# Attention outputs with values as weights, two heads side by side

## The chip, the cores and the metric

The kernel runs on one core of one Trainium2 chip. A core has TensorE (matrix products, PE in the rows), VectorE (DVE), ScalarE (ACT), GpSimd (POOL) and SyncE (SP), which starts most transfers. Each engine works through its own queue in order and waits on semaphores for the others. The metric is the device time of one execution in microseconds; lower is better.

## The reference

A trunk of two layers over 256 latent and 256 context tokens of width 1024. Each layer mixes the tokens in three groups of heads (a state space layer, latent attention, an mLSTM), projects them together (w_out), and then runs 64 experts. The attention group, cut to its core:

```python
def _attend(q_nope, q_rope, k_nope, k_rope, v):
    s = (jnp.einsum('bqhd,bkhd->bhqk', q_nope, k_nope)
         + jnp.einsum('bqhr,bkr->bhqk', q_rope, k_rope))
    p = jax.nn.softmax(s.astype(jnp.float32) * MLA_SCALE, axis=-1).astype(v.dtype)
    return jnp.einsum('bhqk,bkhd->bqhd', p, v)
...
    out_lat = ...          # 256 latent queries over 512 keys (context and latent)
    out_ctx = ...          # 256 context queries over 256 keys, layer 0 only
```

There are 8 heads; a head has 64 + 32 columns of query and key and 64 of value. All is float32.

## The kernel before, in words

A layer is a row of stages. The mixer first projects all inputs; then three generators run woven into each other: `a` is attention (`mla`, L859), `m` the mLSTM (`mlstm`), and `e` the products of a later modulation (`ada_pair`), which stream 1 MB weight tiles from memory. In one round of `weave` (L1379) `a` and `m` take two steps and `e` one; a step is what lies between two `yield`s. The compiler's scheduler then orders the instructions on each engine, and that order is fixed when the program runs. When all three are through, `post` multiplies by w_out (L1429) and the experts follow.

Attention works on items: one head and one segment of 256 queries. A segment has two tiles of 128 queries; the latent one (seg 1) has four tiles of 128 keys, the context one (seg 0) two. In layer 0 there are 16 items, in layer 1 eight (latent only). An item goes through three steps, spread over three turns of the loop at L953:

- `scores` (L906): two products of queries by keys into PSUM, VectorE's maximum along each row (L919), ScalarE's exponential with its row sum (L920), VectorE's reciprocal of the two sums (L921).
- `turn` (L923): TensorE turns each 128 x 128 block of the probabilities (tile `pr` into `pt`), VectorE copies the first query tile out of PSUM and ScalarE the second (L930).
- `outs` (L932): for each key tile and query tile a product with the turned probabilities as weights (128 columns) and the head's 64 value columns moving (L937). The result has queries along the partitions, so the reciprocal sum is one number in each partition: VectorE scales one tile (L944), ScalarE the other (L942), into `on`.

At the end (L970 to L974) the 16 blocks of `on` (8 in layer 1) are turned and copied into `cat`, which w_out reads with features along the partitions.

Names in the rows beside these: `ada` is `e`'s product, four column tiles of the array side by side, each with 32 columns of weights; `st`, `sT`, `mb`, `num`, `int`, `E`, `nd` and `ek` are the mLSTM's (`E` its decay tile of 128 x 512, made from `mb`); `gu` and `dn` are an expert's products; `hT` and `kkT` are other transposes. Transposes stand under L313, the helper `tpose`.

Of the kernel before, what the change touches and what calls it, by code (L numbers as in the profile page):

```python
# [10 lines left out]
F32 = mybir.dt.float32  # L11
BF16 = mybir.dt.bfloat16
I32 = mybir.dt.int32
AF = mybir.ActivationFunctionType
OP = mybir.AluOpType
# [256 lines left out]
class Trunk:  # L272
# [586 lines left out]
    def mla(self, l, qn, kn, kr, mp, cat, last):  # L859
        nc, d, v = self.nc, self.d, self.nc.vector  # L860
# [3 lines left out]
        for j in range(4):  # L864
            (v.tensor_copy if j % 2 else nc.scalar.copy)(kh[j][64:96], kr[64:96])
        V = mp.tile([128, 4, 512], F32, name="V")
        on = mp.tile([128, 4, 512], F32, name="on")
        qh = {}

        def values(i):  # L870
# [28 lines left out]
        def keys(hp):  # L899
            ps = self.bank("kh")  # L900
            nc.tensor.matmul(ps, wkv[:, hp * 128:hp * 128 + 128], kn, start=True, stop=True)
            k2 = kh[2 * (hp % 2):2 * (hp % 2) + 2]
            nc.scalar.copy(k2[0][0:64], ps[0:64])
            v.tensor_copy(k2[1][0:64], ps[64:128])

        def scores(it):  # L906
            h, seg = it["h"], it["seg"]
            nk = it["nk"]
            n = nk * 128
            it["pr"] = pr = mp.tile([128, 2, NT], F32, name="pr", bufs=2)  # L910
            it["sm"] = sm = mp.tile([128, 2, 4], F32, name="sm", bufs=4)
            both = self.bank("s") if nk == 2 else None
            for t in range(2):
                qt = seg * 2 + t
                ps = both[:, t * n:(t + 1) * n] if both is not None else self.bank("s")
                nc.tensor.matmul(ps, qh[h][:, qt * 128:(qt + 1) * 128], kh[h % 4][:, :n], start=True, stop=True)
                it[t] = ps
            for t in range(2):
                v.tensor_reduce(out=sm[:, t, 0:1], in_=it[t], axis=AX.X, op=OP.max, negate=True)  # L919
                nc.scalar.activation(pr[:, t, :n], it[t], AF.Exp, bias=sm[:, t, 0:1], accum_out=sm[:, t, 1:2])  # L920
            v.reciprocal(sm[:, :, 2:3], sm[:, :, 1:2])  # L921

        def turn(it):  # L923
            nk = it["nk"]
            it["pt"] = pt = mp.tile([128, 4, 2, 128], F32, name="pt", bufs=2)
            for t in range(2):
                pp = self.bank("pt")
                for kt in range(nk):
                    self.tpose(pp[:, kt * 128:(kt + 1) * 128], it["pr"][:, t, kt * 128:(kt + 1) * 128])
                (nc.scalar.copy if t else v.tensor_copy)(pt[:, 0:nk, t], pp[:, :nk * 128].rearrange("p (k q) -> p k q", k=nk))  # L930

        def outs(it):  # L932
            h, seg, nk = it["h"], it["seg"], it["nk"]
            po = self.bank("o")
            for kt in range(nk):
                for t in range(2):
                    nc.tensor.matmul(po[:, t * 64:(t + 1) * 64], it["pt"][:, kt, t], V[:, kt, h * 64:(h + 1) * 64],  # L937
                                     start=kt == 0 and t == 0, stop=kt == nk - 1 and t == 1)
            for t in range(2):
                o, a, sc = on[:, seg * 2 + t, h * 64:(h + 1) * 64], po[:, t * 64:(t + 1) * 64], it["sm"][:, t, 2:3]  # L940
                if t:
                    nc.scalar.activation(o, a, AF.Identity, scale=sc)  # L942
                else:
                    v.tensor_scalar(out=o, in0=a, scalar1=sc, scalar2=None, op0=OP.mult)  # L944

        queries(0)
        yield
# [1 line left out]
        for i in range(4):  # L949
            values(i)  # L950
        yield
        items = [dict(h=h, seg=seg, nk=4 if seg else 2) for h in range(8) for seg in ((1,) if last else (1, 0))]
        for n in range(len(items) + 2):  # L953
            if n < len(items):
                h = items[n]["h"]
                if h != items[n - 1]["h"] or n == 0:
                    if h == 4:
                        queries(1)
                        yield
                    if h % 2 == 0 and h < 6:  # L960
                        keys(h // 2 + 1)
                scores(items[n])
                yield
            if 1 <= n <= len(items):
                turn(items[n - 1])
                yield
            if n >= 2:
                outs(items[n - 2])
                yield
        for qt in range(2 if last else 0, 4):  # L970
            ps = self.bank("oT")
            for b in range(4):
                self.tpose(ps[:, b * 128:(b + 1) * 128], on[:, qt, b * 128:(b + 1) * 128])
            (nc.scalar.copy if qt % 2 else v.tensor_copy)(cat[:, 0:4, qt * 128:(qt + 1) * 128], ps.rearrange("p (b n) -> p b n", b=4))  # L974
            yield


# [266 lines left out]
    def mixer(self, l):  # L1244
# [131 lines left out]
        extra = late(extra, pace("late", l, 0))  # L1376
        ml = late(ml, pace("latem", l, 0))
        st = {"m": (ml, x), "a": (mla, y), "e": (extra, z)}
        weave(*(st[k] for k in pace("Do", l, "mae")))  # L1379
        self.dbg(f"cat5{l}", cat5)  # L1380
# [701 lines left out]
```

## Time and profile before

| | us |
|---|---|
| median of three runs | 1956.65 (1954.27 to 1961.2) |
| the profiled execution | 1952.31 |
| its span, first to last instruction | 1950.3 |
| mean granted clock of TensorE | 0.962 |
| TensorE busy | 1792.0 (92%) |
| VectorE busy | 775.7 (40%) |
| ScalarE busy | 394.1 (20%) |

The rows come from the profiled execution. A float32 matmul stands in them as two passes, each with its own weight load (PEld), so the trace counts 320 where the program has 160; a transpose stands as one. Busy time of TensorE holds the time in which a result is still on its way through the array, so the start of the next matmul tells more than the end of this one. The attention stretch of layer 0 ends at 304.2 us, where w_out begins, that of layer 1 at 1337.6.

### The profile page before, as it was taken

The page shows a single profiled execution, that of the slowest core. Times are in us where ns is not written, and L with a number is a line of the kernel's source. Part 1 is how long each engine was busy: PE and PEld are TensorE (multiplying, and loading weights), DVE is VectorE, ACT ScalarE, POOL GpSimd, SP SyncE. Part 2 cuts the span into 40 slices and gives each one's busy share as a digit, 9 for nine tenths or more (in the row PEclk, how much of TensorE's full clock was granted, in tenths as well). Part 3 has the DMA queues.
Part 4 walks back from the last instruction along what each step waited for, and adds up shares of the span by engine and source line. Part 5 has one row for each costly group of instructions (what it writes and reads, how often), then busy time and mean ns, then how long its engine had stood idle before and what let it go on. Part 6 is the DMA issues. An engine that isn't in the chain of part 4 may idle for free. (4 is left out here: it accounts for less than half of the span.)

```text
span 1950.3 us, 29070 instructions
## 1 busy us (share of the span) xinstructions
PE 1792.0 (92%) x10161; PEld 843.7 (43%) x10161; DVE 775.7 (40%) x2252; ACT 394.1 (20%) x756; POOL 453.5 (23%) x453
## 2 busy tenths in 40 slices
PE   6999999979999999999998089899899999999993
PEld 2654665533443433334332056665544444444330
DVE  5656664852422332222221386564722222322113
ACT  2345332301111111111111143531311111011000
POOL 3120211232232232223221570002011111112223
PEclk8999999989999999999999589899899999999997
DMA  8442568299999899999997425258599999996882
GB/s 327 143 98 102 180 242 304 81 337 348 342 335 336 323 304 350 371 352 350 341 365 269 130 74 107 97 217 307 189 417 366 350 345 332 340 370 200 320 296 88
DMA packets 158305, 523.98 MB, mean 269 GB/s; under 512 B 28862, under 2 KB 42110, under 8 KB 149452
## 3 DMA queue, kind: packets, MB, share of 16 engines
q1 hardware_dynamic: 139612, 480.36, 66.6%
q0 software_dynamic: 18544, 41.73, 9.7%
q8 instruction: 82, 1.34, 0.3%
q14 instruction: 67, 0.55, 0.1%
HBM read 531.12 MB, written 47.51 MB: 297 GB/s over the span
## 5 line engine op out<-in xcount | busy, mean ns | idle before, releaser
L1822 PE MATMUL gu<-ring,xT 128*32 128x512 f32 (+3 forms) x2896 | 653.4, 599 | 8.7 <-DMA ring<-in_exp_w 8.6
L1822 PEld LDWEIGHTS gu<-ring,xT 128*32 128x32 f32 (+3 forms) x2896 | 194.2, 128 | 372.0 <-issue 313.0
L1835 PE MATMUL dn<-ring,hT 128*32 128x512 f32 (+3 forms) x1448 | 319.2, 598 | 1.3 <-DVE hT L1726 1.0
L1845 POOL DMA_INDIRECT Y<-xo,gi x79 | 119.9, 1518 | 557.9 <-DMA Y<-xo,gi 129.0
L1718 DVE TENSOR_TENSOR hh<-gu,sg 128x256 f32<-128x256 f32 (+3 forms) x86 | 36.4, 425 | 496.5 <-ACT sg L1717 496.4
L1835 PEld LDWEIGHTS dn<-ring,hT 128*32 128x32 f32 (+3 forms) x1448 | 98.7, 128 | 178.3 <-issue 159.7
L1845 POOL DMA_INDIRECT Y<-xo,si x66 | 90.1, 1365 | 318.0 <-DMA Y<-xo,gi 216.5
L1840 DVE TENSOR_SCALAR xo<-dn,gc 128x512 f32<-128x512 f32 (+3 forms) x80 | 60.1, 751 | 229.5 <-PE dn L1835 221.4
L1717 ACT ACTIVATE sg<-gu 128x256 f32<-128x256 f32 (+3 forms) x86 | 32.8, 384 | 563.4 <-PE gu L1822 545.4
L466 PE MATMUL pT<-hT,w 128*128 128x512 f32 (+1 forms) x288 | 119.1, 566 | 2.5 <-ACT hT L457 2.5
L1797 PEld LDWEIGHTS <-fb 128*128 128x128 bf16 x1536 | 86.5, 99 | 55.0 <-issue 55.0
L1839 ACT ACTIVATE xo<-dn,gc 128x512 f32<-128x512 f32 (+3 forms) x80 | 55.0, 687 | 222.1 <-PE dn L1835 217.6
L1797 PE MATMUL xT<-oneh,fb 128*128 128x128 bf16 (+4 forms) x1536 | 97.3, 220 | 0.0
L1799 ACT COPY xT<-xT 128x512 f32<-128x512 f32 (+3 forms) x80 | 45.8, 573 | 219.4 <-PE xT L1797 137.4
L1429 PE MATMUL yo<-w,cat 128*128 128x512 f32 x192 | 83.3, 593 | 0.7 <-DMA w<-in_w_out 0.7
L1799 DVE COPY xT<-xT 128x512 f32<-128x512 f32 (+3 forms) x80 | 53.4, 670 | 76.5 <-PE xT L1797 43.6
L466 PEld LDWEIGHTS pT<-hT,w 128*128 128x128 f32 x288 | 55.4, 197 | 54.8 <-issue 48.0
L313 PE MATMUL hT<-cst,xt 128*128 128x128 f32 x64 | 14.0, 386 | 61.9 <-DMA w<-in_w_uv 50.8
L1779 POOL DMA_INDIRECT xg<-fd,gi x48 | 51.3, 1068 | 67.6 <-PE xT L313 33.7
L365 PE MATMUL ada<-w,sil 128*32 128x512 f32 x384 | 56.8, 650 | 10.4 <-DMA w<-in_ada_w 10.4
L474 PE MATMUL pN<-w,hT 128*128 128x256 f32 (+2 forms) x256 | 61.0, 395 | 0.0
L313 PEld LDWEIGHTS xT<-cst,xg 128*128 128x128 f32 (+4 forms) x384 | 41.1, 140 | 38.8 <-issue 36.3
(565 smaller groups left out, 2053.1 us busy)
## 6 DMA issues: line engine op xcount, KB each, us to landing
ring<-in_exp_w SPq DMA_DIRECT2D x768, 512.0 KB
w<-in_ada_w SPq DMA_DIRECT2D x48, 1024.0 KB
w<-in_w_out SPq DMA_DIRECT2D x8, 1024.0 KB
sw<-in_sh_w SPq DMA_DIRECT2D x2, 3072.0 KB
w<-in_w_uv SPq DMA_DIRECT2D x4, 1024.0 KB
Y<-zeros SPq DMA_DIRECT2D x8, 512.0 KB
w<-in_w_mm SPq DMA_DIRECT2D x4, 1024.0 KB
w<-in_w_qk SPq DMA_DIRECT2D x4, 768.0 KB
```

The costliest lines, as they stand in the source:

```text
L313: self.nc.tensor.transpose(out, in_, self.c("ident")[:in_.shape[0], :in_.shape[0]])
L365: nc.tensor.matmul(ps[32 * q:32 * q + 32, :], self.sil[:, k, :], t[:, q * 512:(q + 1) * 512], start=k == 0, stop=k == 7, tile_position=(0, ...
L466: self.nc.tensor.matmul(ps[base:base + m, n0:NT], w[k][:, col:col + m], hT[:, k, n0:NT], start=k == 0, stop=k == 7)
L474: self.nc.tensor.matmul(ps[:, :n], hT[:, k, i * 128:(i + 1) * 128], w[k][:, col:col + n], start=k == 0, stop=k == 7)
L1429: nc.tensor.matmul(st[at][n], cb[:, i * 128:(i + 1) * 128], wo[n][b], start=b == 0, stop=b == 7)
L1797: nc.tensor.matmul(o, self.fb[i][:, z, cs], t["oh"][:, i, 0:m], start=at == 0, stop=at + 1 == len(parts))
L1799: (nc.scalar.copy if hh else v.tensor_copy)(o, a)
L1822: nc.tensor.matmul(t["gu"][r, :], t["xt"][:, 2 * c + b, r], ws[j][:, b * 512:(b + 1) * 512], start=c == 0 and b == 0, stop=c == 3 and b == ...
L1835: nc.tensor.matmul(po[n][r, :], t["ht"][:, b, r], ws[b * nr + j][:, n * 512:(n + 1) * 512], start=b == 0, stop=b == 1, **kw)
L1839: nc.scalar.activation(xo[0:m, 0:512], po[0][0:m], AF.Identity, scale=t["gc"][0:m])
L1840: v.tensor_scalar(out=xo[0:m, 512:1024], in0=po[1][0:m], scalar1=t["gc"][0:m], scalar2=None, op0=OP.mult)
L1845: nc.gpsimd.indirect_dma_start(out=self.Y[l], out_offset=bass.IndirectOffsetOnAxis(ap=si[0:cap], axis=0), in_=xo[col:col + cap], in_offset ...
```

## The change

The outputs are computed the other way round. The head's 64 value columns are the weights, and the turned probabilities of both query tiles move, 256 columns. Two heads (2hp and 2hp + 1, `mate`) lie side by side: one fills array columns and PSUM partitions 0 to 63, the other 64 to 127. The result has features along the partitions and queries along the columns, as `cat` wants it, so `on` and the transposes at the end are gone.

The reciprocal sums must now lie along the columns. A new step `sums` does it once for each pair and segment: TensorE turns the four columns of reciprocals `rc` (4 x 128), VectorE copies them to `rT`, four small products with a column of the identity spread over 64 weights copy each row to 64 partitions (`R`), and ScalarE copies `R` out of PSUM. VectorE then multiplies the outputs by `R` straight into `cat`.

Items are ordered by pair, segment and head; `outs` and `sums` come once for each pair, that is on every second item, and `pt` has four buffers instead of two. A `yield` that stood in the loop at the end now ends each turn of the item loop, so attention has more steps, some of them empty.

```diff
--- before.py
+++ after.py
@@ -864,7 +864,6 @@
         for j in range(4):
             (v.tensor_copy if j % 2 else nc.scalar.copy)(kh[j][64:96], kr[64:96])
         V = mp.tile([128, 4, 512], F32, name="V")
-        on = mp.tile([128, 4, 512], F32, name="on")
         qh = {}
 
         def values(i):
@@ -918,30 +917,46 @@
             for t in range(2):
                 v.tensor_reduce(out=sm[:, t, 0:1], in_=it[t], axis=AX.X, op=OP.max, negate=True)
                 nc.scalar.activation(pr[:, t, :n], it[t], AF.Exp, bias=sm[:, t, 0:1], accum_out=sm[:, t, 1:2])
-            v.reciprocal(sm[:, :, 2:3], sm[:, :, 1:2])
+            if it["o"] == 0:
+                it["rc"] = mp.tile([128, 2, 2], F32, name="rc", bufs=2)
+            else:
+                it["rc"] = it["mate"]["rc"]
+            v.reciprocal(it["rc"][:, it["o"]], sm[:, :, 1])
 
         def turn(it):
             nk = it["nk"]
-            it["pt"] = pt = mp.tile([128, 4, 2, 128], F32, name="pt", bufs=2)
+            it["pt"] = pt = mp.tile([128, 4, 2, 128], F32, name="pt", bufs=4)
             for t in range(2):
                 pp = self.bank("pt")
                 for kt in range(nk):
                     self.tpose(pp[:, kt * 128:(kt + 1) * 128], it["pr"][:, t, kt * 128:(kt + 1) * 128])
                 (nc.scalar.copy if t else v.tensor_copy)(pt[:, 0:nk, t], pp[:, :nk * 128].rearrange("p (k q) -> p k q", k=nk))
 
+        def sums(it):
+
+            ps = self.bank("rT")
+            self.tpose(ps[0:4, 0:128], it["rc"].rearrange("p h t -> p (h t)"))
+            rT = mp.tile([4, 128], F32, name="rT", bufs=2)
+            v.tensor_copy(rT, ps[0:4, 0:128])
+            ps = self.bank("R")
+            for t in range(2):
+                for o in range(2):
+                    z = 2 * o + t
+                    nc.tensor.matmul(ps[64 * o:64 * o + 64, t * 128:(t + 1) * 128], self.c("ident", slice(0, 4))[:, z:z + 1].to_broadcast([4, 64]), rT,
+                                     start=True, stop=True, tile_position=(0, 64 * o))
+            it["R"] = mp.tile([128, 256], F32, name="R", bufs=2)
+            nc.scalar.copy(it["R"], ps[:, 0:256])
+
         def outs(it):
-            h, seg, nk = it["h"], it["seg"], it["nk"]
+
+            seg, nk, hp = it["seg"], it["nk"], it["h"] // 2
             po = self.bank("o")
             for kt in range(nk):
-                for t in range(2):
-                    nc.tensor.matmul(po[:, t * 64:(t + 1) * 64], it["pt"][:, kt, t], V[:, kt, h * 64:(h + 1) * 64],
-                                     start=kt == 0 and t == 0, stop=kt == nk - 1 and t == 1)
-            for t in range(2):
-                o, a, sc = on[:, seg * 2 + t, h * 64:(h + 1) * 64], po[:, t * 64:(t + 1) * 64], it["sm"][:, t, 2:3]
-                if t:
-                    nc.scalar.activation(o, a, AF.Identity, scale=sc)
-                else:
-                    v.tensor_scalar(out=o, in0=a, scalar1=sc, scalar2=None, op0=OP.mult)
+                for x in (it["mate"], it):
+                    o = slice(64 * x["o"], 64 * x["o"] + 64)
+                    nc.tensor.matmul(po[o, 0:256], V[:, kt, x["h"] * 64:(x["h"] + 1) * 64], x["pt"][:, kt].rearrange("p t q -> p (t q)"),
+                                     start=kt == 0, stop=kt == nk - 1, tile_position=(0, o.start))
+            v.tensor_tensor(out=cat[:, hp, seg * 256:(seg + 1) * 256], in0=po[:, 0:256], in1=it["R"], op=OP.mult)
 
         queries(0)
         yield
@@ -949,29 +964,29 @@
         for i in range(4):
             values(i)
         yield
-        items = [dict(h=h, seg=seg, nk=4 if seg else 2) for h in range(8) for seg in ((1,) if last else (1, 0))]
+        items = [dict(h=2 * hp + o, o=o, seg=seg, nk=4 if seg else 2) for hp in range(4) for seg in ((1,) if last else (1, 0)) for o in range(2)]
+        for a, b in zip(items[::2], items[1::2]):
+            b["mate"] = a
         for n in range(len(items) + 2):
             if n < len(items):
                 h = items[n]["h"]
-                if h != items[n - 1]["h"] or n == 0:
+                if h % 2 == 0 and items[n]["seg"]:
                     if h == 4:
                         queries(1)
                         yield
-                    if h % 2 == 0 and h < 6:
+                    if h < 6:
                         keys(h // 2 + 1)
                 scores(items[n])
                 yield
             if 1 <= n <= len(items):
                 turn(items[n - 1])
                 yield
-            if n >= 2:
+            if n >= 2 and items[n - 2]["o"]:
                 outs(items[n - 2])
                 yield
-        for qt in range(2 if last else 0, 4):
-            ps = self.bank("oT")
-            for b in range(4):
-                self.tpose(ps[:, b * 128:(b + 1) * 128], on[:, qt, b * 128:(b + 1) * 128])
-            (nc.scalar.copy if qt % 2 else v.tensor_copy)(cat[:, 0:4, qt * 128:(qt + 1) * 128], ps.rearrange("p (b n) -> p b n", b=4))
+            if 1 <= n <= len(items) and items[n - 1]["o"]:
+                sums(items[n - 1])
+                yield
             yield
 
 
```

How the order changes, at three places. Line numbers of the functions behind shift by 15.

TensorE, layer 0, the first items. Before, from the second item's turn on (`pt` is a transpose of probabilities, `o` an output):

```order
L313 MATMUL pt<-cst,pr 128x128 x4
L937 MATMUL o<-V,pt 128x64 x8
L1108 MATMUL st<-va,ek 64x65 x8
L365 MATMUL ada<-w,sil 32x512 x4
L916 MATMUL s<-kh_1349,qh_1371 128x256 x2
L313 MATMUL pt<-cst,pr 128x128 x8
L1108 MATMUL st<-va,ek 64x65 x8
L365 MATMUL ada<-w,sil 32x512 x4
L937 MATMUL o<-V,pt 128x64 x4
```

With the change, about the same place:

```order
L1123 MATMUL st<-va,ek 64x65 x8
L365 MATMUL ada<-w,sil 32x512 x4
L313 MATMUL pt<-cst,pr 128x128 x8
L313 MATMUL rT<-cst,rc 4x128
L945 MATMUL R<-rT,cst 64x128 x4
L1123 MATMUL st<-va,ek 64x65 x8
L365 MATMUL ada<-w,sil 32x512 x4
L915 MATMUL s<-kh_1349,qh_1370 128x256 x2
L1123 MATMUL st<-va,ek 64x65 x8
```

The outputs have moved back behind the second head. Behind the eight transposes stands the turn of the reciprocals (`rT`), and right behind it the four matmuls that need VectorE's copy of it (`R`); the mLSTM's `st` and the next ada group come after them.

VectorE at the same place. Before:

```order
L1088 TENSOR_TENSOR ek<-kk,ex 128x256 x2
L921 RECIPROCAL sm<-sm 128x2
L930 COPY pt<-pt 128x2x128
L944 TENSOR_SCALAR on<-o,sm 128x64
L1116 COPY C_1513<-st 128x65 x2
L1113 SCALAR_TENSOR_TENSOR C_1523<-C_1513,mdec,st 128x65 x2
L1088 TENSOR_TENSOR ek<-kk,ex 128x256 x2
L919 TENSOR_REDUCE sm<-s 128x1
```

With the change:

```order
L918 TENSOR_REDUCE sm<-s 128x1
L1103 TENSOR_TENSOR ek<-kk,ex 128x256
L933 COPY pt<-pt 128x4x128
L924 RECIPROCAL rc<-sm 128x2
L940 COPY rT<-rT 4x128
L1103 TENSOR_TENSOR ek<-kk,ex 128x256
L1128 SCALAR_TENSOR_TENSOR C_1544<-C_1504,mdec,st 128x65 x2
```

The scaling of an output (`on`) is gone from here. The copy of `rT`, for which TensorE waits, stands behind the copy of `pt` and the reciprocal of the second head.

TensorE at the end of layer 0's attention, up to w_out (`yo`). Before:

```order
L313 MATMUL pt<-cst,pr 128x128 x8
L937 MATMUL o<-V,pt 128x64 x4
L365 MATMUL ada<-w,sil 32x512 x4
L313 MATMUL pt<-cst,pr 128x128 x4
L937 MATMUL o<-V,pt 128x64 x8
L365 MATMUL ada<-w,sil 32x512 x4
L937 MATMUL o<-V,pt 128x64 x4
L313 MATMUL oT<-cst,on 128x128 x12
L376 MATMUL adac<-cst,adarow 128x8 x4
L313 MATMUL oT<-cst,on 128x128 x4
L1429 MATMUL yo<-w,cat_108 128x512 x2
```

With the change:

```order
L915 MATMUL s<-kh_1350,qh_2100 128x256 x2
L313 MATMUL pt<-cst,pr 128x128 x8
L313 MATMUL rT<-cst,rc 4x128
L945 MATMUL R<-rT,cst 64x128 x4
L915 MATMUL s<-kh_1351,qh_2103 128x256 x2
L313 MATMUL pt<-cst,pr 128x128 x4
L957 MATMUL o<-pt,V 64x256 x8
L313 MATMUL pt<-cst,pr 128x128 x4
L313 MATMUL rT<-cst,rc 4x128
L945 MATMUL R<-rT,cst 64x128 x4
L957 MATMUL o<-pt,V 64x256 x4
L1444 MATMUL yo<-w,cat_108 128x512 x2
```

In before ada groups lie between the steps up to the end. With the change the ada groups are through, and the last two sums have only attention's own work around them. In layer 1 the end looks like this with the change; there an ada group is cut, one of its four matmuls between `rT` and `R`:

```order
L313 MATMUL pt<-cst,pr 128x128 x8
L957 MATMUL o<-pt,V 64x256 x8
L365 MATMUL ada<-w,sil 32x512 x3
L313 MATMUL pt<-cst,pr 128x128 x8
L313 MATMUL rT<-cst,rc 4x128
L365 MATMUL ada<-w,sil 32x512
L945 MATMUL R<-rT,cst 64x128 x4
L365 MATMUL ada<-w,sil 32x512 x3
L957 MATMUL o<-pt,V 64x256 x8
L1444 MATMUL yo<-w,cat_8117 128x512 x2
```

Of the twelve sums, seven have `R` right behind `rT`; in five an ada matmul or a whole group of four lies between.

## Rows read from the trace of the kernel before

**Rows 1.** Busy us of each engine by stretch, with granted clock and DMA.

```profile
core 0: us, PE busy (x) PEld busy (x) DVE busy (x) ACT busy (x) POOL busy (x), PEclk, DMA share, GB/s
187.00:304.20 117.20, 115.94 (x847) 77.12 (x846) 73.41 (x231) 45.12 (x123) 20.29 (x29) 1.00 0.64 223
1260.00:1337.60 77.60, 76.23 (x556) 48.55 (x554) 46.85 (x137) 27.13 (x65) 11.24 (x18) 1.00 0.59 208
```

**Rows 2.** TensorE waits in both attention stretches: us, times, longest us.

```profile
PE hT L313 <- POOL hs L1194: 0.8, 1, 0.8
...
PE yo L1429 <- DMA w<-in_w_out: 0.7, 1, 0.7
```

**Rows 3.** TensorE in order of time, layer 0 attention: start us, lasting us, work.

```profile
190.45 1.06 PE L365 MATMUL ada<-w,sil 128*32 128x512 f32 x8
191.44 1.09 PE L313 MATMUL pt<-cst,pr 128*128 128x128 f32 x8
192.37 1.88 PE L916 MATMUL s<-kh,qh 96*128 96x512 f32 x4
...
196.55 1.90 PE L937 MATMUL o<-V,pt 128*128 128x64 f32 x16
198.38 0.69 PE L1108 MATMUL st<-va,ek 128*64 128x65 f32 x16
198.99 1.06 PE L365 MATMUL ada<-w,sil 128*32 128x512 f32 x8
```

**Rows 4.** TensorE groups by shape (passes, busy us, mean ns): outputs, both layers.

```profile
L937 PE MATMUL o<-V,pt 128*128 128x64 f32 x192 | 24.0, 275 | 0.0
...
L937 PE MATMUL o<-V,pt 128*128 128x64 f32 x128 | 15.5, 274 | 0.0
```

**Rows 5.** TensorE in order of time, an expert with 64 rows.

```profile
486.68 7.09 PE L1822 MATMUL gu<-ring,xT 128*64 128x512 f32 x32
493.70 1.97 PE L313 MATMUL xT<-cst,xg 128*128 128x128 f32 x16
```

**Rows 6.** VectorE groups by shape, layer 0 attention: count, busy us, mean ns.

```profile
L930 DVE COPY pt<-pt 128x512 f32<-128x512 f32 x8 | 5.5, 686 | 2.3 <-PE pt L313 2.2
L1088 DVE TENSOR_TENSOR E<-mb,amc 128x512 f32<-128x512 f32 x8 | 5.5, 686 | 1.5 <-PE mb L1133 1.5
L944 DVE TENSOR_SCALAR on<-o,sm 128x64 f32<-128x64 f32 x16 | 4.5, 283 | 10.7 <-PE o L937 10.5
L930 DVE COPY pt<-pt 128x256 f32<-128x256 f32 x8 | 3.4, 420 | 1.9 <-PE pt L313 1.9
...
L921 DVE RECIPROCAL sm<-sm 128x2 f32<-128x2 f32 x16 | 2.6, 163 | 1.8 <-ACT pr L920 1.6
```

**Rows 7.** Transposes of probabilities: ns min/median/max, first and last start.

```profile
L313 PE MATMUL pt<-cst,pr x160: 270/273/332, 191.4 to 1325.0; 128*128 128x128 f32 x160
```

**Rows 8.** All engines in order of time, a turn and its copy (w_out stage).

```profile
362.30 1.25 PE L313 MATMUL fT<-cst,f 128*128 128x128 f32 x10
...
362.94 0.59 ACT L1461 COPY pz<-fT 128x512 f32<-128x512 f32 x1 [1.10 <-PE fT L313]
...
363.57 0.55 PE L1463 MATMUL lg<-rw,pz 128*128 128x64 f32 x3
```

**Rows 9.** As rows 1, around a fall of the clock ahead of attention.

```profile
154.27:161.09 6.82, 3.83 (x49) 3.25 (x48) 6.59 (x12) 3.59 (x6) 0.00 (x0) 1.00 0.28 117
161.09:167.92 6.83, 5.84 (x34) 4.65 (x35) 6.49 (x16) 1.68 (x3) 0.00 (x0) 0.50 0.02 4
```

**Rows 10.** TensorE in order of time, the ends of both attention stretches.

```profile
304.20 2.31 PE L1429 MATMUL yo<-w,cat 128*128 128x512 f32 x5
...
1334.10 2.77 PE L365 MATMUL ada<-w,sil 128*32 128x512 f32 x22
1337.61 2.84 PE L1429 MATMUL yo<-w,cat 128*128 128x512 f32 x6 [0.74 <-DMA w<-in_w_out]
```

**Rows 11.** Waits of all engines, layer 0 attention, one of them.

```profile
ACT on L942 <- DVE on L944: 19.0, 15, 2.1
```


## The prediction

> **What bounds the kernel now.** I read the busy time by stretch first, because the share over the whole span mixes stages. In the two stretches in which attention runs, TensorE is busy 115.94 of 117.20 us and 76.23 of 77.60, at the full granted clock, while VectorE has work for about six tenths and the DMA engines for six tenths [rows 1]. Then the waits: over both stretches TensorE's matmul queue waited 0.8 us for GpSimd once and, at the very end, 0.7 us for w_out [rows 2]. So TensorE's own issue is the bound: what is taken from it comes off the time, what is added or made to wait goes on, and what VectorE and ScalarE gain or lose costs nothing unless TensorE stands behind it. The stages behind (w_out, then the experts) are started by the end of these stretches, so I let a shift pass through whole: in layer 0 w_out starts at 304.20, without a wait, and in layer 1 at 1337.61 [rows 10].
>
> The order of TensorE in time gives prices from start to start, which is what a queue pays; a duration holds a tail that overlaps the next. Each float32 matmul stands as two passes. Sixteen passes of outputs, 64 columns moving over 128 of weights, last 1.90 us, but the next group starts after 198.38 - 196.55 = 1.83: 0.114 each; eight transposes take 192.37 - 191.44 = 0.93, 0.116 each [rows 3].
>
> **Removed.** The outputs: 192 passes in layer 0 and 128 in layer 1 [rows 4], at 0.114: 21.9 + 14.6 = 36.5 us. The 24 transposes at the end (16 and 8): 24 x 0.116 = 2.8. Together 39.3 us. The scalings on VectorE and ScalarE and the six copies behind the transposes go too; they are off the path and pay for nothing.
>
> **Added on TensorE.** (a) The outputs are 40 steps over key tiles (4 pairs x (4 + 2), then 4 x 4), each two heads in two halves of the array, two passes, 256 columns moving. The nearest rows are the experts with 64 columns of weights and 512 moving: 32 passes in 493.70 - 486.68 = 7.02 us, so 0.439 for two tiles together, what one tile alone takes for a pass of 512 (six in 2.84 with the tail, in w_out) [rows 5, 10]. Half of that, 0.2195, for 256 columns: 40 x 2 x 0.2195 = 17.6 us. If the two tiles ran one after the other, 35.1.
>
> (b) The sums turned: 12 transposes, 12 x 0.116 = 1.4. (c) The spreading over 64 rows each: 48 matmuls in pairs over the two halves, 128 columns, two passes: 12 x 2 x 2 x 0.116 = 5.6. No row shows a contraction over 4 rows; one after the other it would be 11.1, at the price of the small state pairs (16 passes in 0.61, 0.076 a pair [rows 3]) 3.7. I take 5.6, by columns. (d) Changing the shape of the tile in the array: an ada group (four column tiles, two passes) takes 0.99 us from start to start where its passes are 0.88 [rows 3, 5], so a visit to another shape costs about 0.12. The order shows 12 visits more for the outputs, 2 since two of them are cut by an ada group, and 12 for the sums: 26 x 0.12 = 3.1; nothing if a neighbour has the same shape. (e) The order cuts five ada groups into one and three where it cut two; a cut group pays its passes twice: 3 x 0.88 = 2.6, and the two cut output groups 2 x 0.44 = 0.9. Sum added: 17.6 + 1.4 + 5.6 + 3.1 + 2.6 + 0.9 = 31.2. Without any wait TensorE has 8.1 us less to do.
>
> **The wait that is added.** Each of the 12 sums now goes TensorE, VectorE, TensorE: rT is turned, VectorE copies it, and the spreading matmuls need the copy. In the trace its matmuls start in the order of the program, so behind the waiting one stands all the rest: state, ada, next scores. In the order seven sums have the spreading right behind the turn; in five an ada matmul or a whole group lies between (0.88 or more), which covers it.
> The price of an uncovered one: the last of the four transposes starts at 0.35, is done 0.273 later [rows 7], and the other engine starts some 0.04 after (a turn begins at 362.30, so its fourth transpose ends at 362.92, and ScalarE starts at 362.94; it ends at 363.53, and the next weights load at 363.57 [rows 8]). VectorE copies pt, 0.686, then in its order takes the reciprocal, 0.163 [rows 6]: the turn of rc can start at 0.35 + 0.273 + 0.04 + 0.686 + 0.163 + 0.04 = 1.55, where TensorE had its eight transposes out at 0.93: 0.62 idle. Then 0.273 + 0.04 + a copy of 128 columns (between 0.283 for 64 and 0.420 for 256 [rows 6], I take 0.33) + 0.04 = 0.68, less the 0.116 of its own issue: 0.57 idle. Together 1.19. Where the reciprocal stands ahead of the copy of pt: 0.67; where a decay tile E (0.686 [rows 6]) stands ahead of it, up to 1.3. I take 1.15: 7 x 1.15 = 8.1 us. From below 0.57 each with an empty VectorE, 4.0; from above the longest single wait for VectorE in this stretch, 2.1 [rows 11], on all twelve: 25.2.
>
> **Hidden edits.** The product into cat (128 x 256, 0.42) and ScalarE's copy of R (of the same size) lie beside TensorE's next work and replace more than they add; the product of the last pair is needed by the sixth w_out matmul, 4.4 us on. In layer 1 TensorE waited 0.7 us for w_out since ada's last groups ran back to back at the end, 22 passes from 1334.10 [rows 2, 10]; now scores and outputs lie among them, so w_out's buffers come free earlier: -0.7. If ada still ended last, that stays. In layer 0 the order puts ada ahead and leaves the last two sums without cover; that is in the seven.
>
> **Sum.** -39.3 + 31.2 + 8.1 - 0.7 = -0.7 us on the profiled execution's 1952.3; the median of the three runs is 4.3 above it, so 1956.
>
> **Rivals.** (1) The gain stays: VectorE is idle when the sums come (it has about 37% of the stretch free [rows 1]), the scheduler's neighbours cover the rest: -8.1 - 0.7 = -8.8, 1948. Against it: in seven places nothing independent lies between. (2) Slower, through VectorE's queue: the copy of rT is not just behind pt but behind decay tiles, numerators and reductions that themselves wait for TensorE; each sum then costs up to the 2.1 of [rows 11]: -8.8 + 25.2 = +16.4, 1973. It loses against the kernel before from 0.73 us a sum over all twelve, and by 0.3% from 1.22. For it: VectorE is at 63%; against it: in before TensorE never waited for it measurably. (3) The halves don't run side by side, so the change doesn't do what it says: 35.1 - 17.6 = 17.5 more, 1973; [rows 5] speak against it, with the full factor of two in the same shape of tile. (4) The clock: it fell to 1.2 GHz after a stretch with TensorE busy 3.83 of 6.82 us, and stayed for 6.83 [rows 9], which costs 3.4 of work; the end of layer 0's attention, now without ada, could do that: +3.4, 1959. Against it: with the waits above TensorE is still busy for eight tenths there. (5) The halves overlap only in part: with a fifth of each step lost (a) is 22.0 and the sum 4.4 us worse, 1960; [rows 5] show no such loss at 512 columns, none shows 256.
> The Trainium skill (TensorE: Matmul & The Clock Gate, Part 3, "Measured speedup vs the span model") speaks for (5): it gives a speedup of 2.38 for three column tiles, 0.79 of the ideal. By that share, as an estimate, (a) would be 22.3 and the sum 4.7 us worse. The trace differs: two tiles of 512 columns take as long as one.
>
> **How the numbers follow.** 0.3%, 5.9 us, is about what a measurement of this kernel can tell from no change. Forecast 0.46 (0.40 of it within, 0.03 on either side); (1) 0.22, faster; (2) 0.22, slower; (3) 0.03, slower; (4) 0.04 and (5) 0.03, within. Faster 0.25, same 0.47, slower 0.28. The unknown costs reach from -7.9 (waits of 0.57 on seven, no price for shapes: -8.1 - 3.1 + 4.0 - 0.7) to about +16; 1947 to 1969 leaves out the ends of (1), (2) and (3). The forecast's own range is 1950 to 1962.
>
> **What would show it.** In the profile after: output passes starting in pairs some ns apart, and a group of eight matmuls in about 1.8 us from start to start; between rT and R a gap of about 0.6 us, and about 0.6 before rT, in seven places; attention stretches that together are within 5 us of the 194.8 of [rows 1]; VectorE's busy time nearly unchanged. Wrong if TensorE idles less than 4 or more than 14 us more than before in them, or if outputs take over 25 us.

## The result, and the profile of the changed kernel

The changed kernel takes 1977.71 us (median of 4 runs, 1975.39 to 1981.46), the kernel before beside it 1956.2 (1954.27 to 1961.2): ratio 1.0109, 95% interval 1.0091 to 1.0127. It is slower by 21.5 us where no change was forecast (1956), and above the range (1947 to 1969). The profiled execution took 1976.95 us, span 1975.2, mean granted clock 0.951; before: 1952.31, 1950.3, 0.962. One execution of a later kernel (half of the scalings on ScalarE) took 3074.87 us at a mean granted clock of 0.553, and the ratios leave it out.

First, busy time by stretch, from the first query matmul to the first of w_out: both attention stretches of before (whole, where [rows 1] begin later).

```profile
core 0: us, PE busy (x) PEld busy (x) DVE busy (x) ACT busy (x) POOL busy (x), PEclk, DMA share, GB/s
174.40:304.20 129.80, 128.54 (x885) 82.33 (x881) 79.81 (x247) 53.20 (x138) 20.29 (x29) 1.00 0.60 210
1252.50:1337.60 85.10, 83.73 (x582) 53.39 (x580) 53.89 (x161) 33.44 (x77) 11.24 (x18) 1.00 0.57 206
```

The same two of the changed kernel, and then, in pairs, what lies ahead of a fall of the clock and behind it:

```profile
174.40:318.40 144.00, 138.88 (x844) 76.57 (x840) 80.83 (x244) 51.45 (x129) 20.53 (x29) 0.91 0.61 213
1269.10:1358.60 89.50, 86.99 (x547) 47.65 (x544) 53.86 (x158) 31.96 (x72) 10.45 (x15) 0.92 0.61 217
...
212.10:218.90 6.80, 6.04 (x47) 4.45 (x46) 5.71 (x17) 3.71 (x10) 1.10 (x2) 1.00 0.42 154
218.90:225.70 6.80, 6.80 (x30) 4.24 (x30) 2.87 (x9) 0.63 (x1) 1.95 (x3) 0.50 0.04 6
236.00:242.80 6.80, 5.05 (x45) 3.55 (x45) 4.84 (x18) 2.85 (x8) 3.32 (x6) 1.00 0.84 301
242.80:253.00 10.20, 10.20 (x47) 5.71 (x48) 3.85 (x12) 1.76 (x5) 2.00 (x3) 0.50 0.32 104
266.70:273.50 6.80, 6.09 (x42) 3.84 (x38) 5.90 (x16) 2.50 (x8) 0.00 (x0) 1.00 0.83 277
273.50:283.70 10.20, 10.20 (x42) 5.80 (x45) 5.11 (x20) 2.12 (x6) 1.44 (x2) 0.50 0.60 230
1311.20:1318.00 6.80, 5.87 (x57) 4.58 (x56) 6.46 (x18) 3.19 (x8) 1.16 (x2) 1.00 0.70 288
1318.00:1331.60 13.60, 13.60 (x54) 7.71 (x52) 6.30 (x18) 3.28 (x8) 2.09 (x3) 0.50 0.22 79
```

The stretches grew by 14.2 and 4.4 us, together 18.6 (129.8 + 85.1 = 214.9 before, 233.5 after). The column to read is the granted clock: 1.00 in both before, 0.91 and 0.92 after. It fell to 0.50 (1.2 GHz) four times, for 6.8 + 10.2 + 10.2 + 13.7 = 40.9 us. TensorE was busy all through these and worked at half speed (an ada group of eight passes lasts 1.93 us at 222.44, in the first fall, and 1.07 at 229.77, behind it), so they cost half: 20.4 us. At the full clock the stretches would be 233.5 - 20.4 = 213.1, 1.8 below before. The forecast's sum, without any fall, was -0.7. Length less busy time is TensorE's idle time: 7.6 us in both stretches after, 2.6 before, so 5.0 more. Its work at the full clock is 225.9 - 20.4 = 205.4 us after and 212.3 before, 6.9 less.

Where the falls stand, by TensorE's order of time (start us, lasting us, work, idle time and its releaser in brackets):

```profile
216.13 0.65 PE L313 MATMUL pt<-cst,pr 128*128 128x128 f32 x4
216.62 0.27 PE L313 MATMUL rT<-cst,rc 128*4 128x128 f32 x1
217.66 0.65 PE L945 MATMUL R<-rT,cst 4*64 4x128 f32 x8 [0.76 <-DVE rT L940]
218.24 1.41 PE L1166 MATMUL num<-va,E 128*128 128x65 f32 x8
...
240.93 0.65 PE L945 MATMUL R<-rT,cst 4*64 4x128 f32 x8 [1.75 <-DVE rT L940]
```

Both rows of R are followed by a fall, at 218.9 and 242.8. So are the R at 272.62 (waited 0.71) and 1317.39 (0.93): each fall stands 0.6 to 1.9 us behind the start of an R that had waited for its rT. Not each wait brings one: the R at 311.57 waited 0.83, at 316.85 0.37 and at 199.64 0.58, and the clock stayed. What stands around them differs: the four that are followed by a fall lie beside or between the mLSTM's products (`num`, `int`, `sT`, `mb`), the three others between `ada`, `st`, `s`, `pt` and `o`. No run changed this alone, so whether it decides is not shown. All waits of TensorE in layer 0 (us, times, longest us):

```profile
PE R L945 <- DVE rT L940: 4.4, 5, 1.8
PE glu L812 <- ACT gT L799: 0.9, 1, 0.9
PE R L945 <- ACT pt L933: 0.6, 1, 0.6
```

With layer 1's 0.93 that is 5.9 us in seven places, which compares with [rows 2]; none stands ahead of a turn of rc. The outputs, beside [rows 3]:

```profile
252.38 0.94 PE L313 MATMUL pt<-cst,pr 128*128 128x128 f32 x4
253.26 1.95 PE L957 MATMUL o<-pt,V 128*64 128x256 f32 x16
255.13 1.11 PE L1166 MATMUL num<-va,E 128*128 128x65 f32 x8
```

Sixteen passes in 255.13 - 253.26 = 1.87 us, eight pairs side by side: 0.234 a pair. Outside the two stretches the profiled executions differ by another 6 us; falls there (4.4 us more at 1.2 GHz) are 2.2 of it, and the rest was not traced; the profile of before lies 3.9 under its median, that of after 0.8. Over all fourteen profiles the part between the stretches, from layer 0's w_out to layer 1's first query matmul, takes 947.5 to 957.8 us, so a few us between two medians need not come from attention.

### The profile page after: what moved, and what is told of

Same layout as the page of the kernel before. It is cut to its first block, busy times and chain, and to the rows that moved or that the text cites. A ratio compares the mean times of both kernels' runs of the same rounds, so it can differ in the third digit from the quotient of the medians.

```text
span 1975.2 us, 28906 instructions
## 1 busy us (share of the span) xinstructions
PE 1805.5 (91%) x10085; PEld 832.2 (42%) x10085; DVE 777.5 (39%) x2249; ACT 388.8 (20%) x740; POOL 453.4 (23%) x453
## 5 line engine op out<-in xcount | busy, mean ns | idle before, releaser
L365 PE MATMUL ada<-w,sil 128*32 128x512 f32 x384 | 65.1, 705 | 10.4 <-DMA w<-in_ada_w 10.4
```

The source lines that it names most:

```text
L365: nc.tensor.matmul(ps[32 * q:32 * q + 32, :], self.sil[:, k, :], t[:, q * 512:(q + 1) * 512], start=k == 0, stop=k == 7, tile_position=(0, ...
```

## Experiments

Theory 1: the idle time of TensorE, above all between rT and R, makes the granted clock fall, and that is what was lost. Theory 2: the form of the new matmuls does it (two tiles side by side, or a contraction over 4 rows). Theory 3: no clock, but the chain through VectorE. Length of both stretches together and the time at 1.2 GHz within them, by each profile; each ratio goes by runs of before beside that kernel, with medians of 1955.8 to 1957.9:

| kernel | median us | ratio to before, interval | stretches us | at 1.2 GHz us |
|---|---|---|---|---|
| before | 1956.2 | | 214.9 | 0 |
| changed | 1977.7 | 1.0109 (1.0091 to 1.0127) | 233.5 | 40.9 |
| no sums | 1947.0 | 0.9959 (0.9938 to 0.9981) | 205.3 | 10.2 |
| late spread | 1960.0 | 1.0029 (1.0014 to 1.0044) | 213.2 | 6.8 |
| filled | 1959.9 | 1.0019 (1.0006 to 1.0033) | 219.3 | 3.4 |
| no empty step | 1955.0 | 0.9998 (0.9982 to 1.0014) | 212.8 | 0 |
| before plus sums | 1989.3 | 1.0155 (1.0085 to 1.0225) | 246.9 | 34.1 |
| longer wait | 1982.8 | 1.0132 (1.0115 to 1.0149) | 244.0 | 54.6 |
| division first | 1966.6 | 1.0051 (1.0035 to 1.0066) | 212.7 | 6.8 |
| division first, no empty step | 1950.6 | 0.9967 (0.9951 to 0.9983) | 206.9 | 9.5 |
| no sums, no empty step | 1946.6 | 0.9932 (0.9906 to 0.9958) | 204.4 | 6.8 |

The clock of the other executions agrees with the profiled ones. Its mean was 0.948 to 0.951 in the changed kernel's four, 0.957 to 0.964 in those of before, 0.957 to 0.963 in the ten of "filled", 0.958 to 0.963 in the ten of "no empty step" and 0.946 to 0.951 in the four of "longer wait".

**No sums.** The new outputs alone; the division by the row sums is left out.

```
-            v.tensor_tensor(out=cat[...], in0=po[:, 0:256], in1=it["R"], op=OP.mult)
+            v.tensor_copy(cat[...], po[:, 0:256])
...
-            if 1 <= n <= len(items) and items[n - 1]["o"]:
-                sums(items[n - 1])
-                yield
```

> The change without its round trip for the sums: no rT, no R, the outputs are copied to cat unscaled (the division by the row sums is left out). The new output form stays. Theory 1 (TensorE's idle time between rT and R makes the granted clock fall to 1.2 GHz in the attention stretches; four falls of 40.9 us in all cost about 20 us, the waits 7): no fall in either attention stretch, and with waits, half-clock time and the 7.0 us of work for rT and R gone (12 x 0.116 + 12 x 0.46) about 1978 - 20 - 7 - 8 = 1943 us, 1936 to 1950. Theory 2 (the new output form, two tiles side by side, lowers the clock or is dearer than it looks by itself): falls remain behind the outputs, and only waits and work go: 1962 to 1966.

Measured 1946.95: in theory 1's range, not in theory 2's. But two falls were left, one behind a wait of 2.82 us for GpSimd, one behind 0.94 for VectorE's E, neither right behind an output; theory 1 had expected none.

```profile
175.20:299.40 124.20, 119.59 (x766) 66.35 (x762) 76.99 (x236) 48.12 (x121) 19.76 (x29) 0.99 0.63 222
1250.10:1331.20 81.10, 78.39 (x511) 44.26 (x508) 52.97 (x155) 30.50 (x68) 11.14 (x18) 0.96 0.63 223
```

With half of the 10.2 us taken off, the stretches are 200.2, 14.7 under before. That is not yet what the new form of the outputs is worth, since this kernel waits more than before: TensorE is idle for 205.3 - 198.0 = 7.3 us (2.6 before), though no rT is left to wait for. Its work at the full clock is 198.0 - 5.1 = 192.9 us, 19.4 less than before. The changed kernel is idle as long (7.6) and has 12.5 us more work: that is what the sums cost it beside the clock.

**Late spread.** The same work, the two halves of the round trip put apart.

```
+        def spread(it):
...
+            if n >= 2 and items[n - 2]["o"]:
+                sums(items[n - 2])
+                yield
             if 1 <= n <= len(items):
                 turn(items[n - 1])
...
                 outs(items[n - 2])
+                spread(items[n - 2])
+                finish(items[n - 2])
```

> The round trip is kept and its two halves are put apart: rT is turned behind the next scores, R is spread behind the next turn and the outputs, the product behind R. Nothing is left out. Theory 1 (the wait between rT and R makes the clock fall): few waits over 0.5 us between rT and R, no or one fall in the attention stretches, all work kept: 1978 - 20 - 5 = 1950 to 1958 us. Theory 2 (the form of the new matmuls makes the clock fall, whether TensorE waits or not): the same matmuls, so the same falls, 1970 to 1978. Theory 3 (VectorE's queue, the copies of rT and the product, holds everything up, and the clock is only a sign of it): the copies are as many, 1970 or more.

1960.03, 2 above theory 1's range, 10 below that of the two others. TensorE waits for no rT in its attention stretches any more, and the one fall there (at 275.7) lies in a wait of 2.88 for GpSimd:

```profile
272.11 1.06 PE L365 MATMUL ada<-w,sil 128*32 128x512 f32 x8
276.06 0.69 PE L313 MATMUL hT<-cst,hs 128*128 128x128 f32 x2 [2.88 <-POOL hs L1218]
```

**Filled.** More work, in the place of idle time.

```
             v.tensor_copy(rT, ps[0:4, 0:128])
+            fill = self.bank("fill")
+            nc.tensor.matmul(fill, kn[:, 0:128], wkv[:, 512:], start=True, stop=True)
             ps = self.bank("R")
```

> The change with one independent matmul of 128 x 512 (two passes, into a bank that nobody reads) between rT and R of each of the 12 sums: TensorE works where it waited. It adds 12 x 0.88 = 10.5 us of work in all. Theory 1 (idle time lowers the clock): the waits of 7 us are filled, falls in the attention stretches go, 1978 - 20 - 5 + 10.5 = 1963 us, 1957 to 1968: faster than the changed kernel although it has more to do. Theory 2 (the form of the new matmuls lowers the clock): falls stay, 1978 - 5 + 10 = 1983. Theory 3 (a chain through VectorE bounds the sums, no clock): the filler lies in the waits, 1978 to 1982.

1959.86, in theory 1's range: 18 us faster than the changed kernel, with more to do. TensorE's work at the full clock is 214.75 - 1.7 = 213.1 us, 7.7 more than in the changed kernel (two adaptive groups are cut here, five there, so it is less than the 10.5 of the fillers). The granted clock of the two stretches is 0.99 and 1.00, where it was 0.91 and 0.92:

```profile
174.20:309.70 135.50, 132.66 (x861) 72.56 (x857) 80.62 (x244) 51.33 (x129) 20.56 (x29) 0.99 0.56 195
1262.90:1346.70 83.80, 82.09 (x556) 45.09 (x553) 53.65 (x158) 31.84 (x72) 10.45 (x15) 1.00 0.65 224
```

The one fall left (3.4 us) stands behind a wait of 2.04 for GpSimd. The place of the first fall above, in this kernel:

```profile
216.07 0.27 PE L313 MATMUL rT<-cst,rc 128*4 128x128 f32 x1
216.18 1.02 PE L942 MATMUL fill<-w,kn 128*128 128x512 f32 x2
217.13 0.65 PE L947 MATMUL R<-rT,cst 4*64 4x128 f32 x8
217.72 1.11 PE L1168 MATMUL num<-va,E 128*128 128x65 f32 x8
```

R starts as long after rT as before (1.06 against 1.04 us), but the clock does not fall here. So here it is not the chain's length that lowers the clock, but that TensorE stands idle in it. This is the run that parts theory 1 from both others: the new matmuls are all there.

**No empty step.** One line less, and the scheduler puts adaptive matmuls where TensorE waited.

```
                 sums(items[n - 1])
                 yield
-            yield
```

> The change without the empty step at the end of each turn of the loop over items, in which the scheduler went to the adaptive state between two sums and outputs: in the order an adaptive matmul or group now stands between nearly every rT and R. The work is the same, but for cut groups. Theory 1: the uncovered waits fall from six to one or two, as do the falls of the clock: 1978 - 15 to 20 - 5 = 1953 to 1963 us. Theory 2: the falls stay and the time is 1970 to 1980. Theory 3 (VectorE's queue): the waits stand in another place, behind pt and o, and the time is about 1975.

1955.03, in theory 1's range. Seven of layer 0's eight R now stand behind adaptive passes, as the first here does, and the waits for rT that are left are 0.48 (at the one without) and 0.27:

```profile
198.09 1.04 PE L365 MATMUL ada<-w,sil 128*32 128x512 f32 x2
199.06 0.65 PE L945 MATMUL R<-rT,cst 4*64 4x128 f32 x8
...
269.39 0.27 PE L313 MATMUL rT<-cst,rc 128*4 128x128 f32 x1
270.14 0.65 PE L945 MATMUL R<-rT,cst 4*64 4x128 f32 x8 [0.48 <-DVE rT L940]
```

No fall is left in its stretches, which are 212.8: 2.1 under before, with all matmuls of the change.

```profile
175.40:306.00 130.60, 129.18 (x845) 70.00 (x841) 78.68 (x241) 50.97 (x129) 20.10 (x30) 1.00 0.58 203
1254.40:1336.60 82.20, 80.31 (x547) 44.31 (x544) 54.52 (x160) 31.86 (x72) 10.99 (x18) 1.00 0.61 213
```

The waits have turned into work, though: TensorE is idle for 3.3 us instead of 7.6, and its work is 209.5 us instead of 205.4. Layer 0's adaptive groups are cut into 31 pieces where the changed kernel has 26, and a piece of two passes takes 199.06 - 198.09 = 0.97 us, as long as a group of eight (0.99 in [rows 3]).

**Before plus sums.** The old outputs, with the round trip beside them.

```
+            if it["o"] == 0:
+                it["rc"] = mp.tile([128, 2, 2], F32, name="rc", bufs=2)
...
+            if 1 <= n <= len(items) and items[n - 1]["o"]:
+                sums(items[n - 1])
+                yield
```

> The kernel before with the change's round trip added (rc, rT, R are computed, nobody reads R); outputs stay as they were, with 64 columns moving over one whole array. In the order seven of the 12 R stand right behind their rT, as in the changed kernel. Theory 1 (idle time between rT and R lowers the clock, whatever form the outputs have): 7 us of work, 5 to 7 of waits, and falls of the clock inside the attention stretches that cost 5 to 20 more: 1973 to 1990 us. Theory 2 (the new form of the outputs is needed for the falls): no falls there, 1956 + 7 + 6 = 1969 or less, 1962 to 1970.

1989.31, in theory 1's range. The falls are there without the new outputs, behind R that waited 0.57 and 0.77 us; busy time around the second:

```profile
1308.50:1315.30 6.80, 6.03 (x58) 4.82 (x58) 3.32 (x7) 1.51 (x3) 1.18 (x2) 1.00 0.75 280
1315.30:1342.60 27.30, 27.30 (x114) 19.55 (x114) 12.10 (x33) 5.80 (x15) 3.28 (x6) 0.50 0.19 73
```

Its four runs took 1974.23, 1989.28, 1989.34 and 2003.47 us at mean granted clocks of 0.960, 0.953, 0.952 and 0.945. From first to last the clock's mean is 0.015 lower, which is 0.03 of some 1987 us, 60 us, more at half speed, and so 30 us: the 29 that they differ by. The program is the same, and the clock is enough to account for what parts its runs. Without its 34.1 us at 1.2 GHz it would still be 229.8 - 214.9 = 14.9 above before in the stretches. By busy time 12.3 of that is work (224.6 against 212.3, about as much as the 12.5 that the sums add to the run without them) and 2.6 is idle time (5.2 against 2.6).

**Longer wait.** Two more copies on VectorE.

```
+            for _ in range(2):
+                rw = mp.tile([4, 128], F32, name="rw", bufs=2)
+                v.tensor_copy(rw, ps[0:4, 0:128] if _ == 0 else rv)
+                rv = rw
+            v.tensor_copy(rT, rv)
```

> The changed kernel with two more copies of rT, one after the other, on VectorE: each wait between rT and R grows by some 0.7 us, the work on TensorE is the same. Theory 1 (idle time lowers the clock): 6 uncovered waits bring 4 to 6 us by themselves, and more time at 1.2 GHz in the attention stretches than the 40.9 us of the changed kernel, 50 to 80: 1987 to 2002 us. Theory 3 (the wait is all that is lost): 1982 to 1984. Theory 2 (the form of the matmuls lowers the clock): the 40.9 us stay as they are, 1982 to 1984.

1982.79: by the time theories 2 and 3, 4 below theory 1. By the trace, waits for the sums of 11.0 us (5.9 in the changed kernel) and five falls of 54.6 us in all instead of four of 40.9, each of the five within 2 us of an R that waited 1.3 to 1.8:

```profile
201.90:208.70 6.80, 6.80 (x41) 3.05 (x34) 2.73 (x10) 1.13 (x4) 0.00 (x0) 0.50 0.45 159
222.40:242.90 20.50, 20.50 (x92) 13.48 (x91) 8.95 (x31) 3.68 (x8) 2.77 (x4) 0.50 0.27 83
253.10:259.90 6.80, 6.80 (x31) 4.41 (x28) 1.51 (x5) 0.74 (x2) 1.62 (x2) 0.50 0.16 19
283.80:290.60 6.80, 6.80 (x31) 3.76 (x27) 2.02 (x8) 0.37 (x1) 1.29 (x2) 0.50 0.58 205
1328.30:1342.00 13.70, 13.70 (x56) 8.43 (x60) 5.89 (x16) 2.40 (x7) 2.08 (x3) 0.50 0.24 79
```

Half of the 13.7 more and the 5.1 of waits are 12.0; the stretches grew by 10.5 (three adaptive groups are cut here, five in the changed kernel). The direction is theory 1's, but the profiled run was the slowest of four, and doubling the waits added only a third to the time at 1.2 GHz; waits of 1.33 and 0.96 near the end of layer 0's attention brought no fall. How a wait's length sets a fall is not settled by this.

**Division first.** The probabilities are divided by VectorE before they are turned; no round trip at all. Then the same without the empty step.

```
             v.reciprocal(it["rc"][:, it["o"]], sm[:, :, 1])
+            for t in range(2):
+                v.tensor_scalar(out=pr[:, t, :n], in0=pr[:, t, :n], scalar1=it["rc"][:, it["o"], t:t + 1], scalar2=None, op0=OP.mult)
```

> The change with the division moved ahead: VectorE multiplies the probabilities by the reciprocal sums (a scalar for each query, 48 operations of 128 x 256 or 512) before they are turned; no rT, no R, outputs are only copied to cat. Nothing is left out. Theory 1: TensorE's queue is that of the run without sums, and VectorE has room: 1947 to 1953 us. Theory 3 (VectorE's queue bounds the sums' chain): 48 operations of about 0.42 us are 20 us more on VectorE, and pt waits for them: 1960 to 1970.

> The last kernel without the empty step at the end of each turn of the loop, so that adaptive matmuls stand among the items to the end. Theory 1: waits for the probabilities are covered and no fall of the clock stands in the attention stretches: 3 to 6 us below the last kernel, 1941 to 1949. Theory 3: VectorE's queue decides, the order on TensorE does not: the same as the last kernel within 2 us.

1966.6 and 1950.55. The first misses theory 1's range and has theory 3's time, yet TensorE waited for a scaled pr only once, 0.61 us. Its other waits in layer 0 were 1.92 for the adaptive weights' DMA and 1.38 and 2.60 for GpSimd, and behind none of them did the clock fall. A cause for all of the 16 us between the two kernels was not shown: their profiles differ by 10.7, with 5.8 more in the stretches, 6.9 more between them and 2.0 less elsewhere. The second is 1.6 above theory 1's range, and 16 below the first, where theory 3 had them equal. It is faster than both kernels, by 0.3% against before (and 27 us below the changed kernel), with nothing left out. Its waits in layer 1:

```profile
PE hT L313 <- POOL hs L1207: 4.4, 1, 4.4
PE ada L365 <- DMA w<-in_ada_w: 2.5, 2, 1.9
PE yo L1442 <- DMA w<-in_w_out: 0.6, 1, 0.6
```

The fall that is left (at 1323.5) lies in the first of these.

**No sums, no empty step.** Both edits together: no round trip, and the empty `yield` taken out.

> The run without sums (division by the row sums left out) once more, without the empty step. Theory 1: the two falls of the clock that were left in its attention stretches (10.2 us in all at 1.2 GHz) stood behind waits that the adaptive matmuls now fill: 5 us less, 1939 to 1944. Theory 2 (the new form of the outputs lowers the clock by itself): the falls stay, 1945 to 1950.

1946.6, as with the step: theory 1's 5 us did not come, and the time is in theory 2's range. But no fall stands behind an output. Layer 0's fall went; in layer 1 one of 6.8 us stands in a wait of 4.45 for GpSimd, which the order without the step made longer (it was 1.8 with it).

**Three variants of the best.** Half of the scalings on ScalarE; the empty step in layer 1 alone; both.

```
+            nc.scalar.activation(pr[:, 1, :n], pr[:, 1, :n], AF.Identity, scale=it["rc"][:, it["o"], 1:2])
...
+            if last:
+                yield
```

> The kernel with the division moved ahead and without the empty step, with half of the scalings (the second 128 queries) on ScalarE instead of VectorE. Nothing is left out. Theory 1 (TensorE's queue and its clock decide): VectorE's load is no bound there, so the same as 1950.6 within 3 us. Theory 3 (VectorE's queue makes pt late): 24 operations of 0.3 to 0.6 us leave it, 1940 to 1946.

> The same kernel (division ahead, all on VectorE) with the empty step kept in layer 1 alone, where the runs with it had attention stretches of 80.6 to 84.3 us and those without it 82.2 to 85.8. Theory 1: without it the adaptive weights of the next stage are wanted before their DMA has landed (1.9 us) and TensorE waits 4.4 for GpSimd, and a fall of 13.7 us follows; with it these waits shrink and the fall goes: 1944 to 1949. Against it: the fall only moves to another wait, as in the run with the division ahead and the step kept (6.8 us at 1.2 GHz in layer 1): 1950 to 1955.

> Both edits together: half of the scalings on ScalarE and the empty step in layer 1 alone. If the one helps by VectorE's load and the other by the order in layer 1, 1938 to 1946 us; if neither does, 1948 to 1953.

1954.04, ratio 0.9985 (0.9971 to 0.9999); 1951.8, 0.9981 (0.9967 to 0.9995); 1950.6, 0.9972 (0.9951 to 0.9993). None beats the 0.9967 above. The first is 3.5 above the kernel that it was to equal within 3, and far from theory 3's gain; in the second the fall only moved (to 1289.8, 10.2 us, behind a wait of 1.32 for E). The third has no fall in its stretches, which are the shortest that still divide, 202.8, but its time does not tell it from the others.

## Why the prediction was wrong

**The step that failed is the clock.** The sum holds no term for it, and rival (4) gave it one fall that costs 3.4 us, at "the end of layer 0's attention, now without ada", with a chance of 0.04. Three things in that step were wrong. The place: the falls came in the middle, behind waits for rT, and none at the end. The number: four, of 6.8 to 13.7 us each, 20.4 us lost where 3.4 was priced. And the reason against it, "TensorE is still busy for eight tenths there": ahead of the four falls TensorE was busy 6.04, 5.05, 6.09 and 5.87 of 6.80 us, seven to nine tenths, and the clock fell all the same. The one fall of [rows 9], behind a stretch with 3.83 of 6.82 us busy, was the only one that the prediction went by. Filling the waits, or covering them by another order, took the falls away with the new matmuls in place; the round trip put into the old kernel brought them. The Trainium skill (TensorE: Matmul & The Clock Gate, "A second HAM failure mode: psum-queue depth-cycling") tells of a kernel in which short idle times between groups of matmuls let the clock swing; these traces agree with it (5.9 us of waits in seven pieces, 40.9 at 1.2 GHz), and the prediction did not weigh it.

**The terms of the sum.** At the full clock the stretches are 1.8 below before, where -0.7 was forecast: 6.9 less work (8.1 forecast) and 5.0 more idle time.
- The outputs without the sums: 39.3 off; 17.6, 14 of the 26 visits (1.7) and two cut output groups (0.9) on; and 0.9 off for an ada group, since the run without sums cuts one where before cut two. That is -20.0 forecast; its work is 19.4 less. A pair of passes took 0.234 us for 0.2195: rivals (3) and (5) fell. By the share that the Trainium skill gives (TensorE: Matmul & The Clock Gate, Part 3, "Measured speedup vs the span model"), 22.3 us, a pair would have taken, as an estimate, 22.3 / 80 = 0.279; the measurement decides.
- The sums: 1.4 + 5.6 + 12 visits at 0.12 = 8.4, and four more cut ada groups at 0.88, so 11.9 forecast; 12.5 and 12.3 more work by two pairs of kernels, with and without them. An R lasts 218.24 - 217.66 = 0.58 at the full clock and a turn about 0.12, which is 8.4 for twelve.
- The waits: 8.1 forecast, 5.9 measured, in the seven places of the order. The split was wrong: nothing ahead of the turn of rc, and 0.37 to 1.75 between rT and R where 0.57 each was worked out. In the longest wait rc was turned at 238.91, and VectorE, by the changed kernel's order of time, still had a decay tile E (from 238.77, 0.67 us), a reduction (239.36, 0.41), a copy of pt and a reciprocal in front of rT:

```profile
239.96 0.67 DVE L933 COPY pt<-pt 128x512 f32<-128x512 f32 x1
240.55 0.15 DVE L924 RECIPROCAL rc<-sm 128x2 f32<-128x2 f32 x1
240.62 0.26 DVE L940 COPY rT<-rT 4x128 f32<-4x128 f32 x1
```

- w_out's wait in layer 1 went, as forecast: w_out starts at 1358.64 without one.

Neither of the signs by which the forecast was to be wrong showed: TensorE idled 5.0 us more (under 4 or over 14 was the sign), and the outputs took 80 x 0.234 = 18.7 us (over 25). What failed is the length of the stretches, which was to stay within 5 us and grew by 18.6; the clock, which did that, stands in none of the signs.

**The rivals.** The time came out next to rival (2)'s 1973, but not by its price: VectorE's queue did what it says in the longest wait, and cost 5.9 us in all, not the 25.2 that it rests on. That its time was nearly met is luck. Rival (1), the gain stays, is what would have been left had the waits been covered: "no empty step" covers them and saves 2.1 in its stretches, not 8.8, because the cover is paid for in cut groups (4.1 us more work than the changed kernel).

## What to carry to other kernels

On a queue that has hardly waited, price a new wait twice: by its own length, and by a fall of the clock that may follow it; the falls here cost three times as much as the waits (20.4 us against 5.9). Before moving such a round trip, look in the order for what stands between its two halves, and put independent work there: here even needless matmuls paid. To learn what a part costs, compare busy time as well as length, since the kernel without it can wait elsewhere. Where a change looks slower than its work, compare the granted clock of the stretch before looking for a dearer instruction.

## What was not expected of the hardware

The granted clock fell behind waits as short as 0.57 us. Behind a wait for R it stayed at 1.2 GHz for 6.8 to 27.3 us, although TensorE was busy through all of that. Every fall in the attention stretches of these kernels begins in a wait of TensorE or within 2.5 us after its end. But many waits have none: of the same length, 0.83 and 0.58 in the changed kernel and 0.48 in "no empty step", and longer, 1.92, 1.38 and 2.60 in "division first". The waits for R that were followed by a fall lay beside or between the mLSTM's products in the changed kernel and in "before plus sums"; against that as the whole answer, "longer wait" has a fall at 201.9 behind an R between `pt` and `st`. Which wait brings a fall stays open.
